# S5 steps and opening of a hybrid decoder re-ordered by engine, one gate DMA each way

## The chip, the cores and the metric

The kernel runs on one core of one Trainium2 chip. Its five engines work in parallel, each through its own queue in program order: TensorE (PE, matmuls), VectorE (DVE), ScalarE (ACT), GpSimd (POOL) and SyncE (SP, which issues DMAs; ACT issues some too). The metric is the device time of one launch in microseconds (us).

## What is computed

One inference step of a two-layer decoder over 592 token columns: 16 meta tokens and 512 prompt tokens, then 8 running sequences of 8 tokens. Layer 0 mixes with an S5 state space model, layer 1 with an RG-LRU; each is followed by a gated causal convolution MLP. The part that matters here is the S5 mixer:

```python
u = x @ w_in                                   # 1024 -> 1024
ug = u.reshape(Bsz, L, 64, 16)                 # 64 groups of 16 channels
bu = einsum('blgh,gph->blgp', ug, bb)          # complex, 64 states a group
s  = associative_scan(s_t = a * s_{t-1} + bu_t)   # complex, a is diagonal
y  = Re(einsum('blgp,ghp->blgh', s, c)) + d_skip * u
gy = gelu(y)
vg = gy @ w_out                                # 1024 -> 2048
out = vg[..., :1024] * sigmoid(vg[..., 1024:])
```

The kernel takes time in chunks of 8: it carries the state over 74 chunk starts (66 of the prompt, one for each sequence), and computes what lies within a chunk with a small Toeplitz matrix per group.

## The kernel before

**Matmuls and weights.** Each f32 product is three matmuls of rounded halves (mm3, lines 150 to 154): high times high, low times high, high times low. Weights come in tiles of 128x1024 by `load` on SP (three buffers); ACT makes the high part (whi, L123), DVE the low part (wlo, L132). `project(m, h)` is half a row of the input projection, 24 matmuls of 296 columns; `projected` copies it out on ACT (L448) and, for the second half, issues its DMA to DRAM from ACT's queue.

**A step.** The S5 mixer runs in eight steps, s = 0 to 7, each over eight groups (128 channels). Its pieces are: `flip_b` (PE, L518) and two copies bt on ACT (L520, L521), which expand B; `spread` (PE, L529) and `operators` (DVE, L537), which make the operator xw; `states` (PE, L593), the input of each chunk; `scans` (DVE, L606 to L614), rotation and scan over the chunks; `turned` (DVE, L622 to L627), rotation back; `ends` (two ACT copies, L631, L632), which saves the end states and puts the running sequences' states in; `carries` (POOL, L545), C times powers of A, tile v with two buffers; `lags` (PE, L554, L557) and `windows` (ACT L564, DVE L565, SP L569), which write the Toeplitz entries to DRAM (td); `fetch_lags` (SP, L573), which reads them back as lagged; `assemble` (ACT, L493 to L496), layouts of B and C; `decays` (ACT L579, then POOL); `outputs` (PE L644 with v and the states, then L648 with lagged and u; ACT gelu L652; one DMA of the gate to DRAM on ACT, L654); `fetch_gy` (L660), which reads the gate back in eight DMAs, four on SP and four on ACT; `split_gy` (ACT L674, DVE L675), its high and low part for the output projection. `phases` (DVE) and `tables` (ACT Sin, L478) make the rotations for two steps at a time, with one buffer between them. `bbar` (DVE, L415 to L417) makes B-bar and `turn_b` (PE, L503) transposes it.

**Order.** From line 697 to line 843 the order is written out by hand (`tc.manual_schedule`): each engine works in the order of the program text. An opening (lines 698 to 766) splits x, computes the parameters (`some(n)` issues n of their small DVE operations) and projects rows 0 to 4. In the loop (767 to 811) step s runs states(s) and scans(s), prepares step s+1, then ends(s-1) and outputs(s-1), fetches gate s-2 and splits gate s-3. Behind the loop (813 to 843) the last outputs run between the first matmuls of the output projection (`glu_part`). PSUM has four tiles, 0 to 3, each of which is free again when its last reader is done; `psum(i)` names one. What follows line 843 (GLU, layer norm, MLP, layer 1) isn't changed.

## Time and profile before

| | us |
|---|---|
| median of 3 runs | 1453.86 (1453.37 to 1454.7) |
| the profiled execution | 1456.19 |
| its span | 1454.1 |
| PE busy in it | 1344.7 (92%) |
| DVE busy | 844.1 (58%) |
| ACT busy | 566.9 (39%) |
| POOL busy | 302.3 (21%) |

The profile is one execution, in us from the start of its span; 2.1 us of the execution lie around the span. A timeline row gives start, duration, engine, line, operation, result and sources, how many were merged (x), and in brackets how long the engine had stood idle and what ended that. Durations in the timeline include the fill of the engine, so the start of the next one says more about the pace. The granted clock is 1.00 at 2.4 GHz and 0.50 at 1.2 GHz.

### The profile page before, as it was taken

How to read it: one execution, taken by the hardware profiler on the slowest of the kernel's cores; microseconds unless marked ns; L12 is line 12 of the kernel's file. 1: busy time of each engine (PE TensorE's matmuls, PEld its weight loads, DVE VectorE, ACT ScalarE, POOL GpSimd, SP SyncE). 2: the span in 40 equal slices, each digit the busy share in tenths (PEclk: the TensorE clock that was granted, in tenths of full speed). 3: DMA queues.
4: the chain of work that ended last, by engine and by line, in shares of the span. 5: the costliest groups of instructions: out<-in, count | busy, mean ns of one | idle time of the engine just before them, and what ended most of it. 6: DMA issues, size and time to landing. Idle time of an engine off the chain costs nothing.

```text
span 1454.1 us, 25622 instructions
## 1 busy us (share of the span) xinstructions
PE 1344.7 (92%) x10680; PEld 1320.4 (91%) x10680; DVE 844.1 (58%) x1421; ACT 566.9 (39%) x934; POOL 302.3 (21%) x368
## 2 busy tenths in 40 slices
PE   6658886999899999999999899999999999999995
PEld 5647876999799999999999799998999999999995
DVE  8355663454865434643554988866856335534546
ACT  4333231333544213431433477844534223323433
POOL 2202221234700000000005823146500000000036
PEclk9869767999999999999999999999999999999998
DMA  6223455531132222222222122321222222222211
GB/s 222 70 73 95 122 113 121 164 102 59 54 105 76 87 73 88 71 77 92 81 79 66 59 88 61 103 99 54 92 88 80 81 87 86 66 96 88 77 52 65
DMA packets 80099, 127.66 MB, mean 88 GB/s; under 512 B 30320, under 2 KB 52976, under 8 KB 79984
## 3 DMA queue, kind: packets, MB, share of 16 engines
q1 hardware_dynamic: 65616, 119.24, 26.5%
q10 hardware_dynamic: 14368, 6.79, 1.9%
q8 instruction: 84, 1.38, 0.4%
q14 instruction: 31, 0.25, 0.1%
HBM read 113.35 MB, written 12.66 MB: 87 GB/s over the span
## 4 chain that ended last, share of the span: by engine, by line
PE 76%; DVE 15%; ACT 5%; issue 2%; ACTq 1%; POOL 1%; DMA 0%; DVEq 0%
PE mm L154 23%; PE mm L152 23%; PE mm L153 23%; PE mm L644 3%; DVE wlo L132 1%; PE mm L648 1%; DVE res L945 1%; DVE lo L951 1%; ACTq L660 1%; DVE res L917 1%; PE mm L593 1%; ACT whi L123 1%; DVE tmp L1311 1%; DVE ini L1308 1%; DVE res L940 1%
## 5 line engine op out<-in xcount | busy, mean ns | idle before, releaser
L152 PE MATMUL mm<-hi,whi 128*128 128x296 f32 (+2 forms) x2816 | 848.1, 301 | 32.0 <-ACT bt L521 10.5
L153 PE MATMUL mm<-lo,whi 128*128 128x296 f32 (+2 forms) x2816 | 847.1, 301 | 16.6 <-DVE lo L951 10.1
L154 PE MATMUL mm<-hi,wlo 128*128 128x296 f32 (+2 forms) x2816 | 845.0, 300 | 2.1 <-DVE wlo L132 2.1
L152 PEld LDWEIGHTS mm<-hi,whi 128*128 128x128 f32 x2816 | 537.5, 191 | 35.5 <-ACT bt L521 11.4
L153 PEld LDWEIGHTS mm<-lo,whi 128*128 128x128 f32 x2816 | 537.3, 191 | 24.7 <-DVE lo L951 14.7
L154 PEld LDWEIGHTS mm<-hi,wlo 128*128 128x128 f32 x2816 | 536.8, 191 | 3.4 <-DVE wlo L132 3.4
L132 DVE TENSOR_TENSOR wlo<-wraw,whi 128x1024 fp32r<-128x1024 f32 (+1 forms) x181 | 226.4, 1255 | 219.4 <-ACT whi L123 218.8
L123 ACT ACTIVATE whi<-wraw 128x1024 fp32r<-128x1024 f32 (+1 forms) x188 | 194.6, 1039 | 301.5 <-PE mm L153 293.7
L1133 POOL TENSOR_TENSOR tmp<-tmp,hist 128x16 f32<-128x16 f32 x88 | 20.5, 235 | 697.4 <-DVE tmp L1130 697.4
L1128 DVE SCALAR_TENSOR_TENSOR tmp<-mm,sm,tmp 128x512 f32<-128x512 f32 (+2 forms) x176 | 132.0, 750 | 0.0
L1132 ACT ACTIVATE stg<-mm 128x18 f32<-128x18 f32 x88 | 16.4, 186 | 185.5 <-DVE tmp L1130 185.5
L1180 DVE TENSOR_TENSOR res<-mm,res 128x296 f32<-128x296 f32 (+3 forms) x48 | 26.0, 558 | 80.4 <-PE mm L154 80.4
L1123 ACT ACTIVATE tmp<-mm,sm 128x592 f32<-128x592 f32 (+1 forms) x88 | 72.2, 823 | 0.0
L545 POOL TENSOR_TENSOR v<-cq,ap 128x512 f32<-128x512 f32 x32 | 40.5, 1295 | 79.9 <-PE mm L644 35.8
L1139 DVE TENSOR_TENSOR tmp<-tmp 128x592 f32<-128x592 f32 (+1 forms) x44 | 33.7, 767 | 38.7 <-ACT tmp L1138 38.7
L169 DVE TENSOR_TENSOR lo<-tmp,hi 128x592 fp32r<-128x592 f32 (+2 forms) x48 | 36.6, 763 | 29.6 <-ACT hi L168 29.6
L878 POOL TENSOR_TENSOR s<-s,res 128x296 f32<-128x296 f32 (+2 forms) x45 | 41.8, 931 | 57.3 <-DVE res L1086 27.9
L974 POOL TENSOR_SCALAR res<-res,sm 128x592 f32<-128x592 f32 (+1 forms) x24 | 49.1, 2065 | 7.0 <-DVE lo L951 7.0
L879 POOL TENSOR_TENSOR s<-s,tmp 128x296 f32<-128x296 f32 (+2 forms) x53 | 50.4, 955 | 0.2 <-ACT tmp L874 0.2
L168 ACT ACTIVATE hi<-tmp 128x592 fp32r<-128x592 f32 (+2 forms) x48 | 33.1, 690 | 43.9 <-DVE tmp L1139 30.0
L644 PE MATMUL mm<-sx,v 64*128 64x74 f32 x512 | 40.1, 327 | 10.5 <-ACT sx L632 10.5
L644 PEld LDWEIGHTS mm<-sx,v 64*128 64x128 f32 x512 | 38.7, 239 | 11.9 <-ACT sx L632 11.4
(276 smaller groups left out, 1197.4 us busy)
## 6 DMA issues: line engine op xcount, KB each, us to landing
wraw<-in_wup SPq DMA_DIRECT2D x88, 512.0 KB, 3.4
wraw<-in_wdn SPq DMA_DIRECT2D x32, 448.0 KB, 3.3
wraw<-in_w5o SPq DMA_DIRECT2D x16, 512.0 KB, 4.4
wraw<-in_wdn SPq DMA_DIRECT2D x16, 512.0 KB, 3.6
wraw<-in_wri SPq DMA_DIRECT2D x16, 512.0 KB, 3.5
wraw<-in_w5i SPq DMA_DIRECT2D x8, 512.0 KB, 5.4
td<-lagsb SPq DMA_DIRECT2D x8, 512.0 KB, 3.4
lagged<-td SPq DMA_DIRECT2D x8, 512.0 KB, 4.2
```

Of the source, the lines that this page charges most:

```text
L123: A.activation(hi[:, 0:kk, :], t[:, 0:kk, :], AF.Copy)
L132: eng.tensor_tensor(lo[:, 0:kk, :], t[:, 0:kk, :], hi[:, 0:kk, :].bitcast(F32), op=ALU.subtract)
L152: T.matmul(out, hi[:, k, :], xh, start=start, stop=False)
L153: T.matmul(out, hi[:, k, :], xl, start=False, stop=False)
L154: T.matmul(out, lo[:, k, :], xh, start=False, stop=stop)
L545: G.tensor_tensor(v[:, m], c[:, a, :, None, :].to_broadcast(sh), b[:, NQ * q:NQ * q + NQ, 1:CH + 1, None].to_broadcast(sh), op=ALU.mult)
L644: T.matmul(at_(g, i), v[rows, m, i].rearrange("p d h -> p (d h)"), sx[rows, m // 2, i, 0:NK], start=i + m == 0, stop=False, skip_group_che ...
L878: G.tensor_tensor(self.s1[:, cs_], RES[0][:, cs_] if m == 1 else self.s1[:, cs_], z, op=ALU.add)
L879: G.tensor_tensor(self.s2[:, cs_], self.s2[:, cs_], sq[:, cs_], op=ALU.add)
L974: G.tensor_scalar(z, z, bm, None, op0=ALU.add)
L1123: A.activation(acc[:, d0:NT], X(d0, NT), AF.Identity, scale=w[2], bias=fcb[:, l, m:m + 1])
L1128: V.scalar_tensor_tensor(acc[:, a:TP], X(a - sh, TP - sh), w[k], acc[:, a:TP], op0=ALU.mult, op1=ALU.add)
```

## The change

It re-orders the S5 mixer's opening, loop and end, and alters five things in it:

- flip_b is parted into its matmuls and its two ACT copies (`flipped`), which move to the start of the next step; split_gy is parted into `gy_hi` and `gy_lo`.
- ends(s-1) becomes the first work of step s on ACT; whi, windows, assemble, gate conversions and decays follow it; lags and windows move ahead of outputs.
- v gets the layout (h, d) instead of (d, h), so lags reads it with a step, and the rows of outputs come out as (channel, time in chunk). The matrix read back is put in the same order by a new ACT instruction a step, `toeplitz`; lagged has one buffer instead of two, toe has one.
- The gate is then read back by one DMA on SP instead of eight on SP and ACT.
- PSUM tiles are dealt out anew: projections alternate between 0 and 3, lags moves from 2 to 0, flip_b to 1 for the first three.

In the opening, bbar(2,5) and the weight splits come before other work of their engines, and the projections are placed anew: (5,0) to (6,1) in step 0, row 7 in step 1. At the end, glu_part(0,1) comes after the last outputs.

```diff
-                ps = psum(3 if m < PJ0 and h else 0)[:, 0:HALF]
+                ps = psum((0, 3)[(len(PD) + (m > 4)) % 2])[:, 0:HALF]
+                PD.append(m)
...
                 BT[q] = s5.tile([P, 3, NQ * P], F32, tag="bt", name="bt")
-                pt = psum(0).rearrange("p (r c) -> p r c", r=2)
+                pt = psum(0 if q > 2 else 1).rearrange("p (r c) -> p r c", r=2)
...
+                FL[q] = pt
+
+            def flipped(q):
+                pt = FL.pop(q)
                 A.activation(BT[q][:, 0:2], pt, AF.Copy)
                 A.activation(BT[q][:, 2], pt[:, 1], AF.Copy, scale=-1.0)
...
-                VV[q] = v = s5.tile([P, 4, NQ, CH, 16], F32, tag="v", name="v", bufs=2)
-                sh = [P, NQ, CH, 16]
+                VV[q] = v = s5.tile([P, 4, NQ, 16, CH], F32, tag="v", name="v", bufs=2)
+                sh = [P, NQ, 16, CH]
                 for m, (a, b) in enumerate(((0, apr), (1, api), (0, nai), (1, apr))):
-                    G.tensor_tensor(v[:, m], c[:, a, :, None, :].to_broadcast(sh),
-                                    b[:, NQ * q:NQ * q + NQ, 1:CH + 1, None].to_broadcast(sh), op=ALU.mult)
+                    G.tensor_tensor(v[:, m], c[:, a, :, :, None].to_broadcast(sh),
+                                    b[:, NQ * q:NQ * q + NQ, None, 1:CH + 1].to_broadcast(sh), op=ALU.mult)
...
-                pl = psum(2)
+                pl = psum(0 if q < DM - 1 else 2)
...
-                                 v[:, n, i, 0:CH - 1, :].rearrange("p d h -> p (d h)"), start=n == 0, stop=n == 3)
+                                 v[:, n, i, :, 0:CH - 1].rearrange("p h d -> p d h"), start=n == 0, stop=n == 3)
...
-                lagged = s5.tile([P, NG, P], F32, tag="lagged", name="lagged", bufs=2)
+                lagged = s5.tile([P, NG, P], F32, tag="lagged", name="lagged")
                 nc.sync.dma_start(lagged, TOE[q].rearrange("g p c -> p g c"))
                 TOE[q] = lagged
+
+            def toeplitz(q):
+
+                toe = s5.tile([P, NG, P], F32, tag="toe", name="toe")
+                A.activation(toe.rearrange("p g (h d) -> p g h d", h=16),
+                             TOE[q].rearrange("p g (d h) -> p g h d", d=CH), AF.Copy)
+                TOE[q] = toe
...
-                            T.matmul(at_(g, i), v[rows, m, i].rearrange("p d h -> p (d h)"), sx[rows, m // 2, i, 0:NK],
+                            T.matmul(at_(g, i), v[rows, m, i].rearrange("p h d -> p (h d)"), sx[rows, m // 2, i, 0:NK],
...
             def fetch_gy(q):
-
-                gd = by_group(GD.pop(q)).rearrange("(j h) g k -> g h j k", j=CH)
-                for g in range(NG):
-                    (nc.sync, nc.scalar)[g % 2].dma_start(RES[q][16 * g:16 * g + 16, :].rearrange("p (j k) -> p j k", j=CH), gd[g])
+                nc.sync.dma_start(RES[q], GD.pop(q))
...
-            def split_gy(q, eng=V):
+            def gy_views(q):
+                return RES[q].rearrange("p (j k) -> p k j", j=CH), [t.rearrange("p (k j) -> p k j", j=CH) for t in GY[q]]
+
+            def gy_hi(q):
                 GY[q] = hlpair()
-                gy = RES[q].rearrange("p (j k) -> p k j", j=CH)
-                hi, lo = (t.rearrange("p (k j) -> p k j", j=CH) for t in GY[q])
+                gy, (hi, lo) = gy_views(q)
                 A.activation(hi, gy, AF.Copy)
-                eng.tensor_tensor(lo, gy, hi.bitcast(F32), op=ALU.subtract)
+
+            def gy_lo(q):
+                gy, (hi, lo) = gy_views(q)
+                V.tensor_tensor(lo, gy, hi.bitcast(F32), op=ALU.subtract)
+
+            def split_gy(q):
+                gy_hi(q)
+                gy_lo(q)
...
+            def projection(m, h):
+                project(m, h)
+                projected(m, h)
...
             with tc.manual_schedule():
                 some(24)
@@ -701,133 +713,149 @@
                     if k == 0:
                         load(1)
                         convert_next()
-                    some(2)
+                    some(1)
                     if k == 3:
                         load(2)
                 project(0, 0)
                 convert_next()
+                project(1, 0)
                 for k in range(DM):
                     split_x(k, 1)
-                    some(3)
+                    some(2)
+                load(3)
                 nc.sync.dma_start(bB, s5bc[:, :, 0:128].rearrange("q p (a c) -> p q a c", a=2))
+                projected(0, 0)
+                project(0, 1)
+                projected(1, 0)
+                some(20)
+                convert_next()
+                load(4)
                 nc.sync.dma_start(sp1, s5p[:, S5_COLS["sre"][0]:S5_COLS["sim"][1]].rearrange(
                     "p (r n s) -> p r n s", r=2, s=8))
-                load(3)
+                load(5)
                 fetch_c(0)
                 fetch_c(1)
-                load(4)
-                projected(0, 0)
-                project(0, 1)
+                project(1, 1)
+                projected(0, 1)
+                some(20)
                 convert_next()
-                projected(0, 1)
-                load(5)
-                project(1, 0)
-                projected(1, 0)
-                some(40)
-                project(1, 1)
-                convert_next()
+                some(200)
                 projected(1, 1)
-                some(200)
+                projection(2, 0)
                 bbar(0, 2)
-                project(2, 0)
+                projection(2, 1)
+                load(6)
                 turn(aT, [apw[:, 2 * n:2 * n + 2].rearrange("p q r i j -> p (q r i j)") for n in range(DM // 2)])
-                projected(2, 0)
                 turn_b(0, 2)
                 convert_next()
-                load(6)
-                project(2, 1)
-                projected(2, 1)
+                project(3, 0)
+                flip_b(0)
+                projected(3, 0)
+                flipped(0)
+                spread(0)
                 phases(0)
-                flip_b(0)
-                spread(0)
                 operators(0)
-                project(3, 0)
-                projected(3, 0)
+                convert_next()
+                load(8)
+                project(3, 1)
                 fetch_u(0)
-                fetch_u(1)
                 tables(0)
                 assemble(0)
+                carries(0)
+                decays(0)
+                projected(3, 1)
                 G.tensor_tensor(sm8[:, 0], sp1[:, 0], m8b, op=ALU.mult)
                 G.tensor_tensor(sm8[:, 1], sp1[:, 1], m8b, op=ALU.mult)
-                carries(0)
-                decays(0)
-                project(3, 1)
-                projected(3, 1)
+                bbar(2, 5)
+                assemble(1)
+                flip_b(1)
+                flipped(1)
+                convert_next()
+                fetch_c(2)
                 nc.sync.dma_start(sm, smp)
-                fetch_c(2)
-                convert_next()
-                bbar(2, 5)
-                flip_b(1)
-                assemble(1)
+                projection(4, 0)
                 turn_b(2, 5)
-                project(4, 0)
-                projected(4, 0)
-                project(4, 1)
-                projected(4, 1)
+                projection(4, 1)
                 for s in range(DM):
                     last = s == DM - 1
-                    if s:
-                        run(fetch_u, s + 1)
-                        run(fetch_c, s + 2)
+                    run(ends, s - 1)
+                    run(fetch_u, s + 1)
+                    run(fetch_c, s + 3)
                     load(min(at["conv"] + 3, 12))
-                    states(s)
-                    scans(s)
+                    if 1 < s < DM - 1:
+                        flipped(s + 1)
+                    if at["conv"] < 12:
+                        convert_hi(at["conv"] + 1)
                     if last:
                         lags(s)
                         windows(s)
-                    else:
-                        project_next()
+                    states(s)
+                    if not last:
+                        lags(s)
+                    scans(s)
+                    if not last:
+                        windows(s)
+                    run(assemble, s + 2)
+                    run(toeplitz, s - 1)
+                    run(gy_hi, s - 3)
+                    run(decays, s + 1)
+                    if not last:
                         spread(s + 1)
                         operators(s + 1)
-                        projected_next()
-                    run(ends, s - 1)
+                    fetch_lags(s)
+                    if s == 0:
+                        projection(5, 0)
+                        convert_next()
+                        projection(5, 1)
+                    if s == 1:
+                        projection(7, 0)
                     run(outputs, s - 1)
                     run(fetch_gy, s - 2)
                     turned(s)
-                    if not last:
-                        run(carries, s + 1)
-                        lags(s)
-                        windows(s)
-                    fetch_lags(s)
+                    run(carries, s + 1)
+                    if s == 1:
+                        projection(7, 1)
+                    run(flip_b, s + 2)
                     if at["conv"] < 12:
-                        convert_next()
+                        convert_lo(at["hi"])
                     if s == 0:
+                        flipped(2)
                         phases(1)
                         tables(1)
+                        convert_next()
+                        projection(6, 0)
+                        bbar(5, 8)
                         phases(2)
                         tables(2)
-                        bbar(5, 8)
+                        projection(6, 1)
+                        turn_b(5, 8)
                         phases(3)
                         tables(3)
-                        turn_b(5, 8)
-                    run(flip_b, s + 2)
-                    run(assemble, s + 2)
-                    run(decays, s + 1)
-                    project_next()
-                    projected_next()
-                    run(split_gy, s - 3)
+                    run(gy_lo, s - 3)
                     if s == 6:
                         GL[0, 0] = psum(0), 0
                         glu_part(0, 0, 4, False)
 
                 a, b = DM - 2, DM - 1
-                if at["conv"] < 12:
+                while at["conv"] < 12:
                     convert_next()
+                ends(b)
                 glu_part(0, 0, 5, False)
-                GL[0, 1] = psum(1), 0
-                glu_part(0, 1, 5, False)
-                ends(b)
-                split_gy(a - 1)
+                gy_hi(a - 1)
                 fetch_gy(a)
                 residual(0, 4)
+                toeplitz(b)
                 outputs(b)
+                gy_lo(a - 1)
                 load(15)
+                GL[0, 1] = psum(1), 0
+                glu_part(0, 1, 6, False)
                 GL[1, 0] = psum(2), 0
                 glu_part(1, 0, 6, False)
                 glu_part(0, 0, 6, False)
-                glu_part(0, 1, 6, False)
+                gy_hi(a)
                 fetch_gy(b)
-                split_gy(a)
+                gy_lo(a)
                 GL[1, 1] = psum(3), 0
                 glu_part(1, 1, 6, False)
                 for m in range(2):
```

## Rows read from the trace of the kernel before

**Rows 1.** Windows: stretch, its length, each engine's busy us (instructions), granted clock, DMA share, GB/s.

```profile
133.30:235.30 102.00, 84.05 (x1186) 78.72 (x1184) 60.91 (x74) 28.75 (x80) 27.15 (x30) 0.77 0.45 106
235.30:262.90 27.60, 19.48 (x197) 18.68 (x198) 6.89 (x12) 3.61 (x6) 0.00 (x0) 0.81 0.64 173
262.90:349.70 86.80, 86.80 (x638) 86.56 (x637) 40.82 (x89) 32.41 (x52) 26.09 (x29) 1.00 0.32 102
```

**Rows 2.** Chain of waits, 200 to 212 us: start, us, what.

```profile
201.95 0.38 ACTq L654
...
205.86 0.92 ACT bt L520
...
208.99 1.10 ACT hi L674
...
210.28 0.27 ACT sx L632
```

**Rows 3.** Timeline of PE, then of DVE and ACT, in the opening and step 0.

```profile
64.07 0.87 PE L503 MATMUL mm<-ident,bb 128*128 128x128 f32 x3 [11.38 <-DVE bb L417]
...
95.24 0.88 PE L503 MATMUL mm<-ident,bb 128*128 128x128 f32 x3 [11.26 <-DVE ph L461]
...
86.56 0.16 DVE L461 COPY ph<-pv 128x8 int32<-128x8 int32 x1
...
98.47 1.33 ACT L478 ACTIVATE res<-pc 128x296 f32<-128x296 int32 x2
```

**Rows 4.** Timeline of PE, step 1 (full clock), then step 6.

```profile
113.37 3.80 PE L644 MATMUL mm<-sx,v 64*128 64x74 f32 x64
117.10 2.01 PE L648 MATMUL mm<-u,lagged 128*128 128x74 f32 x16
...
119.18 0.95 PE L557 MATMUL mm<-v,bst 128*32 128x112 f32 x32
120.06 1.16 PE L518 MATMUL mm<-bB,sel 64*128 64x128 f32 x16
...
204.57 2.27 PE L593 MATMUL mm<-u,xw 128*64 128x74 f32 x64
...
210.60 6.85 PE L644 MATMUL mm<-sx,v 64*128 64x74 f32 x64 [2.66 <-ACT sx L632]
217.38 3.69 PE L648 MATMUL mm<-u,lagged 128*128 128x74 f32 x16
```

**Rows 5.** Timeline of DVE in step 0 (one row) and step 5, then of POOL.

```profile
83.69 0.46 DVE L627 TENSOR_TENSOR sx<-t 128x296 f32<-128x296 f32 x1
...
189.95 1.19 DVE L675 TENSOR_TENSOR lo<-res,hi 128x592 fp32r<-128x592 f32 x1 [3.01 <-ACT hi L674]
...
197.34 0.77 DVE L622 TENSOR_TENSOR t<-t,res 128x592 f32<-128x592 f32 x1
198.03 1.63 DVE L623 TENSOR_TENSOR t<-t,res 128x592 f32<-128x592 f32 x1
...
200.82 1.31 DVE L627 TENSOR_TENSOR sx<-t 128x296 f32<-128x296 f32 x1
...
197.63 5.42 POOL L545 TENSOR_TENSOR v<-cq,ap 128x512 f32<-128x512 f32 x4 [8.59 <-PE mm L644]
```

**Rows 6.** The page's groups: busy us, mean ns of one, idle before.

```profile
L132 DVE TENSOR_TENSOR wlo<-wraw,whi 128x1024 fp32r<-128x1024 f32 (+1 forms) x181 | 226.4, 1255 | 219.4 <-ACT whi L123 218.8
...
L168 ACT ACTIVATE hi<-tmp 128x592 fp32r<-128x592 f32 (+2 forms) x48 | 33.1, 690 | 43.9 <-DVE tmp L1139 30.0
```

**Rows 7.** Windows of 2 us, columns as in rows 1.

```profile
122.00:124.00 2.00, 0.96 (x7) 0.96 (x8) 0.98 (x1) 1.99 (x9) 0.00 (x0) 1.00 1.11 268
...
206.00:208.00 2.00, 1.94 (x44) 1.66 (x38) 1.12 (x1) 1.99 (x8) 0.00 (x0) 1.00 0.99 266
```

**Rows 8.** The page's DMA issues: count, KB of one, us to landing.

```profile
td<-lagsb SPq DMA_DIRECT2D x8, 512.0 KB, 3.4
lagged<-td SPq DMA_DIRECT2D x8, 512.0 KB, 4.2
```

More of the change, by code (lines that the diff above doesn't have):

```diff
@@ L34 @@
 CENTER = 4
-PJ0 = 5
 S5_COLS = dict(lre=(0, 32), lim=(32, 64), ls=(64, 96), dsk=(96, 104), sre=(104, 360), sim=(360, 616),
@@ L426, in trunk @@
                 G.memset(t[:, :, :, 0:1], 0.0)
+            PD = []
             U, XW, CC, BST, VV, BT, TOE = {}, {}, {}, {}, {}, {}, {}
-            UT, UD, GD, PJ, PH, D0, ST = {}, {}, {}, {}, {}, {}, {}
+            UT, UD, GD, PJ, PH, D0, ST, FL = {}, {}, {}, {}, {}, {}, {}, {}
             def by_group(dram):
@@ L685, in convert_next @@
                 convert_lo(at["conv"] + 1)
-            proj = [(m, h) for m in range(PJ0, DM) for h in (0, 1)]
-            def project_next():
-                if proj:
-                    project(*proj[0])
-            def projected_next():
-                if proj:
-                    projected(*proj.pop(0))
+            def projection(m, h):
+                project(m, h)
+                projected(m, h)
             with tc.manual_schedule():
```

## The prediction

> **What bounds the kernel now.** I first cut the span into stretches. From 262.9 us on TensorE (PE) is full: 638 matmuls in 86.8 us, so 0.136 us for one of 296 columns and 3.3 us for the 24 of half a projection [rows 1]. The diff touches nothing there, so whatever is won must be won before 262.9. In the recurrence, 133.3 to 235.3, PE is busy for 84 of 102 us, but at a mean granted clock of 0.77, so much of that busy time is itself stretched [rows 1]. I mark the steps by the first matmul of outputs (L644), which belongs to the step before: from 133.3 to 235.3 five steps took 102.0 us, 20.4 each [rows 1].
>
> The chain of waits says what a step is made of. After the gate's gelu, ScalarE (ACT) issues the gate DMA at 201.95 and four fetches behind it, then works through the next steps' conversions: bt at 205.86, assemble, decays, hi of split_gy at 208.99. Only then come the two copies of ends, at 210.28 [rows 2], and only they let PE go on. So the step is ACT's 9 us and PE's 10.5 us in series: outputs waits for ends, ends stands at the tail of ACT's queue, and that queue was blocked until outputs' gelu. Before the steps PE stands still twice for transposes of bbar, for 11.38 and 11.26 us [rows 3].
>
> **The opening.** The first stop is bbar(2,5), which on VectorE (DVE) is queued behind a weight split, whose whi stands behind tables(0) on ACT; it also runs beside carries on GpSimd (POOL). The change puts that split before tables(0), and bbar(2,5) behind it on a DVE that is then free: I take back 11.4 us. Project (2,1) moves into PE's 2.3 us wait before the first turn_b, and the projections after the first stop no longer run at half clock for their first 3 us (1.6 us). Sum: 15 us, states(0) at about 57. The parameter arithmetic that keeps DVE busy until 33 us has the same instructions, so splitting x with one parameter step between instead of two wins nothing here. The sm8 products move behind carries(0) on POOL; they then end near 57, when scans(0) is ready: nothing, or 2 us.
>
> In step 0 the phases on DVE and the Sin tables on ACT still take turns, since they share one buffer: 86.56 to 99.80 in the trace, 13.2 us [rows 3]. Interleaved with two weight splits and four projections, I count 19 us from turned(0) at 68.5, so 87.4. Behind it ACT does ends(0), whi, windows, assemble, toeplitz, decays and the copy of project(7,0), 6 us: outputs(0) may start at 93, not 113.4 [rows 4]. **Gain to here 20 us.** Until outputs(1), PE has L644 3.7, L648 1.95, project(7,1) 3.3, flip 1.1, then bt(3) on ACT 1.5, lags 1.2 and spread 1.1, like flip's 1.1 [rows 2, 4], plus about 1 for semaphores: 15 us against 19.9, 5 us. PE has however just idled before outputs(0); at half clock L644 and L648 take 6.85 and 3.65 [rows 4]. I keep half of it: 1.5 us. **Gain 21.5 us.**
>
> **A steady step.** Let T be the end of turned(s-1). ACT does ends first (T+0.5), then bt(s+1) (T+2.0). PE has done states(s); lags(s) needs the PSUM tile that bt frees, so it runs T+2.0 to 3.3, spread to 4.4, L644 to 8.1, L648 to 10.1, flip to 11.2, states(s+1) to 13.4 [rows 4]. DVE does the two low parts, scans, the windows' small operation, operators, turned. Of these, scans to turned took 191.1 to 202.1 in the trace, 11.1 us; low part of the gate 1.2 [rows 5], the small one 0.2, and while weights are still being split 1.2 more [rows 6]: starts overlap by a tenth, so 13.6 us in two steps, 12.4 in three. So DVE becomes the bound, with PE idle for 2.3 us or less in one piece: five steps are 2 x 13.6 + 3 x 12.4 = 64.4 us instead of 102.0, **37.6 us**.
>
> Costs inside. toeplitz adds one ACT instruction of 128x1024 with 64-byte steps: hi of the gate, also strided, takes 1.10 for 592 elements [rows 2], the packed hi 0.69 [rows 6], so 1.2 to 1.9 for 1024. I take 1.9, since it is strided too; ACT then ends it at about T+6.6, under L644, which ends at 8.1: nothing. Its cover gone, it costs up to 1.9 a step. The moving operand of lags now has 32-byte steps; no row prices PE for that. By the same two rows it is 1 to 1.6 times 0.95 [rows 4], or 0 to 0.6 us more, within PE's idle time: nothing. The one gate fetch takes four issues off ACT, some 2.2 us a step, and is on SP behind fetch_lags, which waits for td; gy_hi comes a step later, so nothing waits. carries still begins when L644 frees v [rows 5], and lags(s+1) needs it at L644's end + 5.5; flip and states cover that. Its four products have other broadcast axes but the same 512 elements, and fetch_c and load are as many issues on SP as before, ahead of td: nothing each.
>
> carries meets turned as it does now: L623 took 1.63 us beside POOL and its twin L622, begun before POOL, 0.77; L627 1.31 against 0.46 in step 0. With L626 like L627 that is 2.5 of turned's 4.8 us [rows 5]. The 4.8 stands in the sum; if carries drifts off, it is 2.5 less a step, 12 in all. The Trainium skill (SBUF — State Buffer, Who interferes with whom) states that one of a VectorE operation with two SBUF inputs and a GpSimd one that reads SBUF blocks fully until the other has finished. Four operations each waiting for a whole carries instruction of 1.3 us would make turned 7.1 us and five steps 11 us longer; the row, with 4.8, shows less. As a rival it gives 1409.
>
> **The clock** is the largest unknown. PE kept 1.00 through an idle 1.8 us, from flip's end at 121.2 to 123.0 [rows 4, 7], but 2.66 us before 210.60 sufficed for a cold L644 [rows 4]. A step's gap of 2.3 us lies between. A drop costs 3.1 on L644, 1.7 on L648 and, until states, some 1.3 more: 6 us. For five steps I allow 1.5 drops, 9 us, which leaves 28.5.
>
> **The end.** outputs(6) to the end of outputs(7) is 27.6 us now [rows 1]. After: 5.7 for outputs(6), 2 until gate 4's low part, 0.8 for glu, 5.7 for outputs(7), 1.9 waiting for toeplitz(7): 16.1. glu_part(0,1) with its 30 matmuls moves behind it, 4.1 us. 27.6 - 16.1 - 4.1 = 7.4, of which I keep 6. The fetches of gates 6 and 7 are hidden: 18.8 us of other glu matmuls follow. The four-tile output tail named in the change's words has no line in the diff: nothing.
>
> **Sum:** 21.5 + 28.5 + 6 = 56 us. The profiled execution took 1456.2 (span 1454.1 and 2.1 around it), 2.3 over the median of 1453.9. 1456.2 - 56 - 2.3 gives **1398 us**. With no drop it is 70 us (1384), with turned uncontended 80 (1374).
>
> **Rivals.**
> (1) The clock falls in every step. PE is then the bound: 6.85 + 3.65 for outputs, 4.6 for lags and spread at twice their rows, then warm 1.1 for flip and 2.2 for states, 18.4 a step [rows 4], so 92 instead of 102; with 21.5 before and 3 after, a gain of 34.5, 1419 us. For it: a gap near the critical length in every step; against: the clock was up again by 206, after flip and states [rows 7], and they now run straight on into lags and spread. The Trainium skill (TensorE: Matmul & The Clock Gate, HAM oscillation) describes a kernel whose bursts between waits each start throttled.
> (2) The round trip td to lagged to toeplitz bounds the step: lagged now has one buffer, and on ACT gelu and the next ends stand behind toeplitz. 3.4 and 4.2 us to landing [rows 8] and 1 for the two issues, from T+6.6: T+15.2, while toeplitz is reached at T+13.6+4.7. Slack 3 us; if both landings double, 4.5 us are lost in each of five steps: 1420.
> (3) The other side: PE stays at half clock from the opening to outputs(7). Each step is then 21.6 us of PE work (10.5, twice 1.2, 1.1, 1.1 and 2.2), over the present 20.4, and half a projection 6.6. From 47 us on, where project(3,1) ends, that is 8 halves, 53 us, 8 steps, 173, and 10 for glu and transposes: outputs(7) ends at 283, with the moved 4.1 us 24 later than now: 1478. It decides only if the projections stay cold too; against it speaks that they ran at 1.00 just before 124 [rows 7].
>
> **How the numbers follow.** Forecast 0.67, drops in every step 0.16, the port 0.06, the round trip 0.05, slower 0.04, nothing moved 0.02. Range 1374 to 1428: the bound of the forecast below; above, rivals 1 and 2 and 8 us more, should my count of step 0 be short by two in five. A measurement tells about 0.2% (3 us): faster 0.94, same 0.02, slower 0.04.
>
> **What would show it.** Right: ends just behind turned on ACT, L644 spaced 12 to 14 us, DVE busy over 80% there, no four ACT fetches, PE's wait before L644 gone. Wrong: L644 of 6.9 us in most steps (1), L648 waiting for toeplitz over 3 us (2), states(0) after 65 us (opening).

## The result, and the profile after

The changed kernel takes 1402.9 us (median of four runs, 1398.4 to 1412.4), the kernel before in the same rounds 1454.3 us: a ratio of 0.966, with a 95% interval of 0.961 to 0.971. A second set of five runs gave 1410.7 us against 1456.6, 0.968 (0.965 to 0.971). The forecast was 1398 us, within 1374 to 1428. The profiled execution of the changed kernel took 1403.1 us, its span 1401.3; that of before 1456.2 and 1454.1, so 53.1 us went. The nine runs of the changed kernel lie in two groups, at 1398 to 1403 and at 1411 to 1412 us; where a difference below is taken from 1402.9, it is some 8 us smaller against the second set.

The line numbers have moved: outputs is L656 and L660 now, states L605, lags L559 and L562, spread L534, flip L519, ends L643 and L644, bt L525 and L526, hi and lo of the gate L685 and L689, the weights' whi and wlo L122 and L131, toeplitz L584, the four products of turned L634 to L639, carries L550.

The windows of the trace, with the columns of [rows 1], cut where the prediction cut them: states(0) to outputs(0), to outputs(1), to outputs(6), to the end of outputs(7).

```profile
54.14:91.82 37.68, 30.59 (x397) 27.69 (x396) 31.59 (x65) 22.33 (x51) 6.57 (x9) 0.95 0.43 139
91.82:114.01 22.19, 21.68 (x249) 20.28 (x249) 4.93 (x10) 6.32 (x15) 4.26 (x4) 0.69 0.27 72
114.01:185.52 71.51, 62.86 (x1114) 56.60 (x1112) 60.64 (x72) 36.42 (x78) 28.87 (x30) 0.98 0.54 140
185.52:203.90 18.38, 16.67 (x171) 16.07 (x167) 8.47 (x13) 5.51 (x8) 0.00 (x0) 0.75 0.66 210
```

The third row answers the first of [rows 1]: the same five steps take 71.5 us instead of 102.0, VectorE (DVE) works for 60.6 us of it as against 60.9, now 85% of the stretch, and TensorE's (PE's) granted clock is 0.98 instead of 0.77. The second row is the one that got worse: PE is busy for all but 0.5 us, at a mean clock of 0.69.

ScalarE (ACT) in a steady step, as a timeline; it answers [rows 2]:

```profile
140.61 1.99 ACT L584 ACTIVATE toe<-lagged 128x1024 f32<-128x1024 f32 x1
142.51 1.24 ACT L685 ACTIVATE hi<-res 128x592 fp32r<-128x592 f32 x1
...
145.79 0.73 ACT L664 ACTIVATE gu<-mm 128x296 f32<-128x296 f32 x2 [1.70 <-PE mm L660]
146.55 0.43 ACTq L666 DMA_DIRECT2D gd<-gu  x1
150.37 0.27 ACT L643 ACTIVATE hold<-sx 128x72 f32<-128x72 f32 x1 [3.85 <-DVE sx L639]
150.66 0.26 ACT L644 ACTIVATE sx<-sp 128x64 f32<-128x64 f32 x1
150.83 1.01 ACT L525 ACTIVATE bt<-mm 128x1024 f32<-128x1024 f32 x1
151.73 0.59 ACT L526 ACTIVATE bt<-mm 128x512 f32<-128x512 f32 x1
```

ends (L643) here waits for turned's last product on DVE, and for nothing on its own queue: ACT has 3.85 us to spare in front of it. In step 5 it stands behind gelu and the gate DMA and starts at 162.30, 2.2 us after turned's end at 160.13. What trailed at the end of ACT's queue leads it, with bt behind.

DVE and GpSimd (POOL) at the same place, and the two low parts of the step before, against [rows 5] and [rows 6]:

```profile
134.91 2.13 DVE L131 TENSOR_TENSOR wlo<-wraw,whi 128x1024 fp32r<-128x1024 f32 x1
136.96 2.07 DVE L689 TENSOR_TENSOR lo<-res,hi 128x592 fp32r<-128x592 f32 x1
...
145.41 0.77 DVE L634 TENSOR_TENSOR t<-t,res 128x592 f32<-128x592 f32 x1
146.09 1.67 DVE L635 TENSOR_TENSOR t<-t,res 128x592 f32<-128x592 f32 x1
147.79 1.25 DVE L638 TENSOR_TENSOR sx<-t 128x296 f32<-128x296 f32 x1
148.97 1.36 DVE L639 TENSOR_TENSOR sx<-t 128x296 f32<-128x296 f32 x1
150.25 1.18 DVE L689 TENSOR_TENSOR lo<-res,hi 128x592 fp32r<-128x592 f32 x1
...
158.49 0.77 DVE L635 TENSOR_TENSOR t<-t,res 128x592 f32<-128x592 f32 x1
...
144.32 5.69 POOL L550 TENSOR_TENSOR v<-cq,ap 128x512 f32<-128x512 f32 x4
...
159.69 5.45 POOL L550 TENSOR_TENSOR v<-cq,ap 128x512 f32<-128x512 f32 x4
```

Three of turned's four products are stretched beside carries, to 1.67, 1.25 and 1.36 us, as in [rows 5]; the first, L634, is not, though by the profile carries has begun. The low parts now run beside carries too in some steps, 2.13 and 2.07 us where 1.2 was in the sum. In step 5 turned is all but done when carries begins at 159.69; L635 then takes 0.77 us and turned 2.3 in all.

PE from outputs(3) to outputs(4), against [rows 4], and the transposes of the opening, against [rows 3]. Here and in the expectations a step is named by the outputs at its end, so this is step 4:

```profile
50.44 0.49 PE L504 MATMUL mm<-ident,bb 128*128 128x128 f32 x3
...
77.93 0.52 PE L504 MATMUL mm<-ident,bb 128*128 128x128 f32 x3 [4.01 <-DVE ph L462]
...
140.02 3.80 PE L656 MATMUL mm<-sx,v 64*128 64x74 f32 x64
143.74 2.01 PE L660 MATMUL mm<-u,toe 128*128 128x74 f32 x16
145.68 1.16 PE L519 MATMUL mm<-bB,sel 64*128 64x128 f32 x16
146.77 2.27 PE L605 MATMUL mm<-u,xw 128*64 128x74 f32 x64
152.37 0.32 PE L559 MATMUL mm<-cq,bst 128*32 128x16 f32 x16 [3.33 <-ACT bt L526]
152.52 1.82 PE L562 MATMUL mm<-v,bst 128*32 128x112 f32 x32
154.27 1.16 PE L534 MATMUL mm<-aT,sel 32*128 32x128 f32 x16
155.36 3.80 PE L656 MATMUL mm<-sx,v 64*128 64x74 f32 x64
```

The first transposes wait for nothing (11.38 us before), the second for 4.01 (11.26). In the step, outputs no longer waits; the wait stands before lags, which needs the PSUM tile that bt frees. It is 3.33 us here, the longest such wait, and the next outputs still takes 3.80 us, that is, at full clock. The windows say the same, against [rows 7]; the third is the whole of step 5:

```profile
148.00:150.00 2.00, 1.05 (x34) 0.89 (x28) 2.00 (x2) 0.00 (x0) 2.00 (x2) 1.00 1.14 233
150.00:152.00 2.00, 0.00 (x0) 0.00 (x0) 2.00 (x3) 1.60 (x4) 0.01 (x1) 1.00 1.26 214
...
155.36:167.30 11.94, 11.94 (x226) 10.76 (x225) 9.36 (x15) 7.68 (x15) 5.57 (x6) 1.00 0.61 166
```

In step 5, with turned undisturbed, PE is busy for all 11.94 us at full clock and DVE for 9.36: that step is PE's. The three before it are DVE's, which is busy for 13.3 of 13.6, 12.4 of 12.5 and 14.9 of 15.3 us.

The page's DMA issues give td 3.4 and lagged 4.2 us to landing, as in [rows 8].

**Where the 53 us are.** Up to outputs(0) 113.37 - 91.82 = 21.6; to outputs(1) 19.9 before and 22.2 now, so 2.3 back; five steps 102.0 - 71.5 = 30.5; outputs(6) to the end of outputs(7) 27.6 - 18.4 = 9.2, of which 4.1 are matmuls that moved behind it, so 5.1. That is 55; 2 us are lost again later, which I have not followed.

### The profile page after: what moved, and what is told of

Same layout as the page of the kernel before. It is cut to its first block, busy times and chain, and to the rows that moved or that the text cites. A ratio compares the mean times of both kernels' runs of the same rounds, so it can differ in the third digit from the quotient of the medians.

```text
span 1401.3 us, 25545 instructions
## 1 busy us (share of the span) xinstructions
PE 1333.1 (95%) x10680; PEld 1308.4 (93%) x10680; DVE 840.2 (60%) x1421; ACT 582.7 (42%) x942; POOL 301.1 (21%) x368
## 4 chain that ended last, share of the span: by engine, by line
PE 76%; DVE 17%; ACT 4%; issue 2%; POOL 1%; DMA 0%; SPq 0%; DVEq 0%; ACTq 0%
PE mm L152 24%; PE mm L153 24%; PE mm L151 24%; DVE wlo L131 2%; DVE res L973 1%; DVE lo L979 1%; PE mm L656 1%; DVE xw L542 1%; DVE res L945 1%; PE mm L660 1%; PE mm L605 1%; DVE t L635 1%; ACT res L479 1%; DVE res L968 1%; ACT whi L122 1%
## 5 line engine op out<-in xcount | busy, mean ns | idle before, releaser
L131 DVE TENSOR_TENSOR wlo<-wraw,whi 128x1024 fp32r<-128x1024 f32 (+1 forms) x181 | 228.2, 1265 | 220.0 <-ACT whi L122 219.3
L122 ACT ACTIVATE whi<-wraw 128x1024 fp32r<-128x1024 f32 (+1 forms) x188 | 194.5, 1039 | 302.5 <-PE mm L152 297.5
L906 POOL TENSOR_TENSOR s<-s,res 128x296 f32<-128x296 f32 (+2 forms) x45 | 41.8, 930 | 60.9 <-DVE res L1114 31.2
L550 POOL TENSOR_TENSOR v<-cq,ap 128x512 f32<-128x512 f32 x32 | 42.5, 1359 | 49.8 <-ACT cq L494 41.1
L902 ACT ACTIVATE tmp<-res 128x296 f32<-128x296 f32 (+2 forms) x56 | 24.0, 445 | 58.0 <-DVE res L1208 24.7
L1206 DVE SCALAR_TENSOR_TENSOR res<-res,mm 128x592 f32<-128x592 f32 (+1 forms) x16 | 12.2, 762 | 59.2 <-PE mm L153 59.2
```

Source lines behind the costliest of these rows:

```text
L122: A.activation(hi[:, 0:kk, :], t[:, 0:kk, :], AF.Copy)
L131: eng.tensor_tensor(lo[:, 0:kk, :], t[:, 0:kk, :], hi[:, 0:kk, :].bitcast(F32), op=ALU.subtract)
L550: G.tensor_tensor(v[:, m], c[:, a, :, :, None].to_broadcast(sh), b[:, NQ * q:NQ * q + NQ, None, 1:CH + 1].to_broadcast(sh), op=ALU.mult)
L906: G.tensor_tensor(self.s1[:, cs_], RES[0][:, cs_] if m == 1 else self.s1[:, cs_], z, op=ALU.add)
```

## The experiments

**Is the lead of ends enough, and is it needed?** The prediction's main step was that outputs waits for ends and ends stands at the tail of ACT's queue. First only that was moved, in the kernel before (step 7 has a call of its own behind the loop):

```diff
-                    run(ends, s - 1)
                     run(outputs, s - 1)
                     run(fetch_gy, s - 2)
                     turned(s)
+                    if not last:
+                        ends(s)
```

> The kernel before with one edit: ends(s) is issued right behind turned(s), so on ScalarE it stands ahead of that step's weight, bt, assemble, decays and gate copies instead of behind them. Theory A (the step was ScalarE's 9 us and PE's 10.5 us in series because ends stood at the queue's tail): a step becomes VectorE's sum of some 13.6 us instead of 20.4; over six steps about 40 us less, 1414 us, with PE's wait before the outputs gone. Rival (the position of ends matters only together with the other moves, since bt, the eight fetches or the cold clock set the step just as well): steps stay near 18 us or more and the time above 1438 us.

Measured: 1451.1 us, 0.997 of before (0.996 to 0.998). The rival holds; 5 us of 53 come. The trace (line numbers of before) shows the wait before outputs gone and the ring closed elsewhere. ACT, DVE and PE in step 5, in order of time:

```profile
188.87 1.23 ACT L674 ACTIVATE hi<-res 128x592 fp32r<-128x592 f32 x1
...
190.13 1.20 DVE L675 TENSOR_TENSOR lo<-res,hi 128x592 fp32r<-128x592 f32 x1 [3.33 <-ACT hi L674]
...
200.85 0.42 PE L554 MATMUL mm<-cq,bst 128*32 128x16 f32 x16 [6.23 <-DVE xw L537]
...
202.98 0.27 ACT L631 ACTIVATE hold<-sx 128x72 f32<-128x72 f32 x1 [7.61 <-DVE sx L627]
```

ACT's tail still holds hi of the gate; DVE has the gate's low part ahead of scans and waits 3.33 us for hi; so scans, operators and turned are late, lags waits 6.23 us for operators, since lags and spread share a PSUM tile, and ends itself waits 7.61 us for turned. Moving one instruction out of a serial ring shows the next one in it.

Then the reverse, in the changed kernel: ends behind toeplitz, hi and decays on ACT, everything else new.

```diff
                 for s in range(DM):
                     last = s == DM - 1
-                    run(ends, s - 1)
...
                     run(gy_hi, s - 3)
                     run(decays, s + 1)
+                    run(ends, s - 1)
```

> The changed kernel with ends(s-1) moved behind bt, whi, windows, assemble, toeplitz, the gate's high part and decays on ScalarE, everything else as it is. Theory A: the outputs' first matmul begins some 4.5 us later in each step, steps go from about 13.5 to 17 or 18 us, 1428 to 1435 us. Rival (the gain is the other re-ordering): within 5 us of the changed kernel, 1400 to 1408 us.

Measured: 1451.0 us, 0.997 (0.996 to 0.999). All of the gain but 5 us is gone, and more than theory A allowed: the lead of ends is necessary. The copies it was put behind are some 5 us of ACT, but the steps are 21 to 24 us, for PE now waits 1.7 to 4.5 us in front of outputs and, but for the last of them, comes back at half clock:

```profile
140.12 7.11 PE L656 MATMUL mm<-sx,v 64*128 64x74 f32 x64 [4.46 <-ACT sx L644]
...
150.78 2.08 PE L519 MATMUL mm<-bB,sel 64*128 64x128 f32 x16
152.80 3.88 PE L605 MATMUL mm<-u,xw 128*64 128x74 f32 x64
```

From outputs to flip every matmul is at half speed, and most of states (7.11 against 3.80, 2.08 against 1.16, 3.88 against 2.27). This is what rival (1) described. The Trainium skill (TensorE: Matmul & The Clock Gate, HAM oscillation) tells of bursts that each start throttled; these rows agree.

**What the gate's new way is worth.** The new order with the old v layout, no toeplitz, two lagged buffers, and eight gate fetches, alternately from SyncE (SP) and ACT:

```diff
-                nc.sync.dma_start(RES[q], GD.pop(q))
+                gd = by_group(GD.pop(q)).rearrange("(j h) g k -> g h j k", j=CH)
+                for g in range(NG):
+                    (nc.sync, nc.scalar)[g % 2].dma_start(RES[q][16 * g:16 * g + 16, :].rearrange("p (j k) -> p j k", j=CH), gd[g])
```

> The changed kernel with the old layout of v, two buffers for lagged, no toeplitz, and the gate fetched in eight DMAs again; the new order stays. Theory A (VectorE bounds the step, so none of this lies on its path): steps within 0.5 us of the changed kernel, a few us lost at the end where the last two gates are fetched: 1400 to 1408 us. Rival (four fetch issues on ScalarE, 2.2 us a step, still hold up the next ends): 1415 us or more. The other way: lags with a packed operand takes 0.95 us instead of 1.82 and toeplitz's 1.95 us is gone; if these were on the path it would be 1390 us.

Measured: 1426.0 us, 0.980 (0.978 to 0.983), 23 us above the changed kernel's 1402.9 and 15 above its second set: the rival. ACT's timeline shows why:

```profile
142.03 0.38 ACTq L666 DMA_DIRECT2D gd<-gu  x1
142.45 6.10 ACTq L671 DMA_DIRECT2D res<-gd  x4
148.60 0.27 ACT L643 ACTIVATE hold<-sx 128x72 f32<-128x72 f32 x1 [6.60 <-DMA res<-gd]
```

The four issues hold ACT's queue for 6.10 us here and for 2.2 to 6.6 us in the other steps, and ends is what stands behind them. Three of the five outputs that follow run at half clock. To tell the issues from the transfers and from the layouts, one word was changed in that kernel, all eight issues to SP:

```diff
-                    (nc.sync, nc.scalar)[g % 2].dma_start(
+                    nc.sync.dma_start(
```

> As e3_old_gate (the layouts, buffers and eight gate fetches of before inside the new order), but all eight fetches are issued by SyncE, none by ScalarE. Theory A (in e3 the four issues on ScalarE stood between gelu and ends for 6.1 us, and with ends leading, all of it fell on the path that sets the end: that is what e3 lost): 1398 to 1410, ends within 1.5 us of gelu. Rival (it is the eight transfers themselves, or the eight issues wherever they stand, since SyncE now holds td and lagged behind them): 1418 or more.

Measured: 1405.8 us, 0.967 (0.965 to 0.969), between the changed kernel's two sets. ends follows the gate DMA at once:

```profile
137.12 0.38 ACTq L666 DMA_DIRECT2D gd<-gu  x1
137.82 0.27 ACT L643 ACTIVATE hold<-sx 128x72 f32<-128x72 f32 x1 [0.73 <-ACT gu L664]
...
130.82 11.91 SPq L671 DMA_DIRECT2D res<-gd  x8
```

On SP the eight issues may take 11.91 us and cost nothing that the runs can tell. So 20 us were four DMA issues on the wrong queue, half clock that followed from them included. The one large gate DMA, the transposed v and toeplitz together are worth no more than that one word, as far as the runs can tell; one by one they weren't tried, and since this kernel's lags is packed too, gains and losses among them could cancel. The Trainium skill (DMA: Bandwidth & Descriptors, Rules for kernel authors) says that spreading DMAs over several engines saves only the issuing time; here the issuing time decided.

**The strided operand of lags, and the clock.** In the changed kernel lags reads v with 32-byte steps and takes 1.82 us, not 0.95 [rows 4]. Packed again:

```diff
-                                 v[:, n, i, :, 0:CH - 1].rearrange("p h d -> p d h"), start=n == 0, stop=n == 3)
+                                 v[:, n, i].rearrange("p h d -> p (h d)")[:, 0:P - 16], start=n == 0, stop=n == 3)
```

> The changed kernel, but lags reads the first 112 elements of v packed instead of with a step of 32 bytes (so the entries within a chunk are in the wrong order; the amount of work is the same). Expected: the 32 matmuls of lags take 0.95 us instead of 1.82. Theory A (hidden in PE's idle time, VectorE bounds the step): 0 to 3 us less, 1400 to 1403 us. Rival (they lie on the path of every step): 7 us less, 1396 us.

Measured: 1415.6 us (1408.8 to 1416.0), 0.971 (0.968 to 0.974). Both theories missed: with less work, the kernel is some 13 us slower than the first set of the changed kernel and 5 slower than the second; one of its four runs (1408.8) lies within the range of those nine. lags does take 0.95 us, but:

```profile
124.68 0.32 PE L559 MATMUL mm<-cq,bst 128*32 128x16 f32 x16 [2.80 <-ACT bt L526]
...
128.26 7.11 PE L656 MATMUL mm<-sx,v 64*128 64x74 f32 x64
...
143.85 0.95 PE L562 MATMUL mm<-v,bst 128*32 128x112 f32 x32
```

bt comes from DVE and ACT and is ready when it was; PE just arrives earlier, idles for 2.80 us instead of 1.54, and the next outputs runs at half clock. Two of the five steps are cold so. My new theory: the step is DVE's, PE's spare time is paid for in clock. Two runs test it, the changed kernel once more and the packed lags issued twice:

> The changed kernel as it is, on the same chip and in the same rounds as the three edits beside it, so that a few microseconds between them can be read. Theory A (its time moves with the number of stretches at half clock): 1398 to 1412 over its runs, and those with a lower mean granted clock are the longer ones. Rival (the spread has another source, for example transfers): the mean clock of the runs doesn't order their times.

> As e4_lags_packed (the lags' moving operand packed, so its entries within a chunk are in the wrong order), but the 32 packed matmuls are issued twice, first into columns of the same PSUM tile that nobody reads. TensorE's time for lags is then 2 x 0.95 = 1.9 us a step, as the strided ones took (1.82), and nothing else differs from e4. Theory A (e4 was slower only because TensorE, with 0.9 us less to do in a step that VectorE sets, idled longer and came back at half clock): 1398 to 1407, at least 8 us under e4's 1415.6, TensorE's clock at 1.00 between outputs(1) and outputs(6). Rival (something else in the packed reading costs e4 its 12 us, and work that nobody needs only adds time): 1415 or more.

```diff
+                for to in (pl[:, 512 + 16:512 + P], pl[:, 16:P]):
                     for n in range(4):
                         for i in range(NQ):
-                            T.matmul(pl[32 * i:32 * i + 32, 16:P], bst[:, n // 2, i, :],
+                            T.matmul(to[32 * i:32 * i + 32], bst[:, n // 2, i, :],
```

Measured: packed lags twice, 1404.1 us (1402.4 to 1405.7), 0.965 (0.963 to 0.966). Useless work on PE took 11 us off. One expectation was too neat: the clock did fall once after a wait for bt, of 3.21 us, but was up again before outputs. The changed kernel's second set gave 1410.7 us. Its nine runs form two groups: four of 1398.4 to 1403.1 us with a mean clock of 0.980 to 0.984, five of 1410.7 to 1412.4 with 0.973 to 0.976. The profiled execution of the second set belongs to the longer group, and its step 4 has the very wait of the first:

```profile
153.87 0.32 PE L559 MATMUL mm<-cq,bst 128*32 128x16 f32 x16 [3.33 <-ACT bt L526]
154.02 1.82 PE L562 MATMUL mm<-v,bst 128*32 128x112 f32 x32
155.77 2.08 PE L534 MATMUL mm<-aT,sel 32*128 32x128 f32 x16
157.78 7.11 PE L656 MATMUL mm<-sx,v 64*128 64x74 f32 x64
```

The steps before it agree with the first trace to 0.1 us, and the wait is 3.33 us in both. Once the clock stayed, once it fell, and then outputs(3) to outputs(5) took 16.3 and 18.6 us instead of 15.3 and 11.9. So the same wait cost 8 us or nothing, by something that neither trace shows. The run with eight issues on SP has both cases in one execution, two steps apart:

```profile
122.71 0.32 PE L559 MATMUL mm<-cq,bst 128*32 128x16 f32 x16 [2.62 <-ACT bt L526]
...
155.54 0.32 PE L559 MATMUL mm<-cq,bst 128*32 128x16 f32 x16 [2.63 <-ACT bt L526]
```

After the first, outputs took 7.11 us, after the second 3.80. A gap of that length can't be priced as hit or miss from one profile. That this wait makes the whole second group was seen in one profile of it only; the runs below, with a shorter wait, bear it out.

**The opening.** One part of it undone, the weight split after operators(0) put behind tables(0) again:

```diff
                 operators(0)
-                convert_next()
...
                 projected(3, 1)
+                convert_next()
```

> Undo of one part of the opening: the weight split that follows operators(0) stands behind tables(0) and the copy of projection (3,1) again, ahead of bbar(2,5), as it did before the change. Theory A (this order is what took TensorE's 11.4 us wait for bbar(2,5) away): states(0) 8 to 12 us later than 54.1, total 1410 to 1415. Rival (the wait went because bbar(2,5) now precedes the split of the next weights and GpSimd's carries, so that the split's place matters little): states(0) within 4 us of 54.1, total 1400 to 1407.

Measured: 1416.4 us, 0.971 (0.968 to 0.973), against 1410.7 and 0.968 (0.965 to 0.971) for the changed kernel in the same rounds. The intervals overlap, but both kernels have two groups of runs, and each of this one lies some 6 us above that of the other: 1407.6 against 1401.2, 1416.6 against 1410.7; a fifth run, 1410.9, lies between them. PE's transposes and states(0):

```profile
56.14 0.88 PE L504 MATMUL mm<-ident,bb 128*128 128x128 f32 x3 [5.53 <-DVE bb L416]
```

A wait of 5.53 us is back, and states(0) begins at 62.1, 6.4 later than at 55.6 in the changed kernel beside it. It lies between the two theories: the place of the split explains about half of the 11.4 us that I gave to it.

**A version that beats both.** Two stretches of the changed kernel still idle: the transposes of bbar(5,8) in step 0 (4.01 us, above), and step 6, where glu_part(0,0) waits for the low part of gate 3, 3.35 us, and step 6 takes 18.2 us.

```diff
                         projection(6, 1)
+                        projection(7, 0)
                         turn_b(5, 8)
...
-                    if s == 1:
-                        projection(7, 0)
...
-                        glu_part(0, 0, 4, False)
+                        glu_part(0, 0, 3, False)
```

> Two edits for the two stretches in which the changed kernel still falls to half clock or idles. First: project(7,0) stands ahead of the transposes of bbar(5,8) in step 0 instead of ahead of outputs(0) in step 1. Second: in step 6 glu_part(0,0) takes three gates instead of four, so that it doesn't wait for the low part of gate 3. Theory A: outputs(0) begins at 86 to 88 instead of 91.8, with less of it at half clock, and step 6 is 4 us shorter: 1388 to 1395. Rival (project(7,0) only moves from one place that TensorE must fill to another, VectorE's scans and turned set the time of outputs(1), and glu's matmuls come back behind outputs(7)): 1400 to 1406.

Measured: 1399.8 us (1392.9 to 1401.3), 0.960 (0.958 to 0.963), 10.8 below the changed kernel in the same rounds, a little less good than expected and again in two groups. To fill the wait for bt with work that is needed, spread was put ahead of lags:

```diff
                     states(s)
                     if not last:
+                        spread(s + 1)
                         lags(s)
...
                     if not last:
-                        spread(s + 1)
                         operators(s + 1)
```

> One move in the changed kernel: spread(s+1), which TensorE issues behind lags(s), stands ahead of it, so that its 1.16 us fall into TensorE's wait for bt (1.52 us in step 2, 3.33 us in step 4) and no longer behind it. Theory A (the 8 us between the changed kernel's runs are one fall to half clock after the 3.33 us wait of step 4; a shorter wait is not followed by one): all runs 1396 to 1405, no cluster at 1410. Rival (the clock falls by some other cause, or spread now holds back lags, windows and the round trip behind them): runs at 1410 still, or all above 1405.

> The same move on top of e7_both (project(7,0) earlier, three gates in step 6), whose runs lay at 1393 to 1394 and at 1400 to 1401. Theory A: all runs 1387 to 1395. Rival as for e10_spread_first: runs at 1400 still.

> e11_both_spread with the second half of project (7,1) in step 2 instead of step 1. In e7_both outputs(0) to outputs(1) took 22.2 us, with VectorE idle for 12.3 of them, since TensorE had outputs(0) and this half at half clock ahead of states(2). Theory A (the step that follows outputs(0) is TensorE's, the ones behind it are VectorE's, so 3.3 to 6.6 us of TensorE's work move from the one to the other's slack): 4 to 6 us under e11_both_spread. Rival (TensorE has no 3.3 us to spare in step 2, or its wait for the copy of the projection costs as much): within 2 us of e11_both_spread or above.

Measured, with before at 1455.9: spread alone 1395.8 us (1394.6 to 1398.1), 0.959 (0.958 to 0.960); on top of the two edits 1387.6 (1386.8 to 1388.4), 0.953 (0.952 to 0.955); with project(7,1) in step 2 besides 1385.5 (1383.5 to 1387.5), 0.952 (0.951 to 0.953). The second group is gone in all three, in four or five runs each. The same wait in step 4 of the first of them, and the five steps of the last:

```profile
146.16 0.32 PE L559 MATMUL mm<-cq,bst 128*32 128x16 f32 x16 [1.73 <-ACT bt L526]
```

```profile
101.72:166.93 65.21, 63.79 (x1134) 57.10 (x1130) 59.77 (x72) 36.00 (x82) 30.41 (x30) 1.00 0.58 157
```

3.33 us became 1.73, and the five steps take 65.2 us at a clock of 1.00, with project(7,1) in them. Part of the gain of spread lies in the opening: outputs(0) takes 3.80 us there instead of 6.56. The last move gave 2.1 us where 4 to 6 were expected; its interval overlaps that of the run it builds on, so it isn't shown to be faster than it.

## Why the prediction was right, point by point

- **Outputs waits for ends, ends at the tail of ACT's queue.** Right, but as half of the cause. With the other changes ends' lead is worth 48 us (1451.0 against 1402.9; 40 against the second set), alone it is worth 5. The prediction's own ring for the new step had the other conditions in it (low part behind scans, lags in another PSUM tile, ACT without the four issues), and it took them as given. Of these only ACT's issues were tried by themselves.
- **The gate fetches, "some 2.2 us a step off ACT ... nothing waits".** This step was wrong in kind. The four issues took 2.2 to 6.6 us a step in the new order, and once ends leads they stand right before it: 20 us. The sum came out because the new step was built without them; the part's own worth was put at nothing.
- **Opening, 20 us to outputs(0).** 21.6 measured; states(0) at 54.1, not 57, outputs(0) at 91.8, not 93. Of the 11.4 us for the split's place 6.4 were shown. As to the rest, bbar(2,5) itself took 6.1 us on DVE before, beside carries, 3.7 with the split late and 2.1 in the changed kernel; this wasn't tried apart.
- **outputs(0) to outputs(1), 1.5 us kept.** Wrong in sign, -2.3. outputs(0) took 6.56 us and project(7,1) ran cold behind it; the drop that I halved came in full in both profiled executions of the changed kernel. (Half of the 5 us would also have been 2.5, not 1.5.)
- **Five steps, 64.4 us of DVE and 9 for the clock.** 71.5 measured, 73.4 forecast, by other parts: the near hit is partly luck. DVE is the bound, as said, in steps 2 to 4; scans to turned took 11.3 us in steps 2 and 4, against 11.1. Step 5 is PE's, 11.9 us. The steps were 13.6, 12.5, 15.3, 11.9 and 18.2 us, not all 12 to 14. The clock fell in the profiled execution only in step 6; in the profile of the longer group it cost 8 us more, so the 9 us stand as an upper end. Instead two steps grew, step 4 to 15.3 us, since low parts beside carries took 2.1 us for 1.2, and step 6 to 18.2, since glu waited for gate 3's low part.
- **turned beside POOL.** 5.05 us against 4.8 in the sum where it met carries, and not the 7.1 of that rival: 1.67 us for L635 beside carries, 0.77 before it. carries is stretched too: its four products take 4.26 us at 98.46, where DVE is idle, and 5.69 here, so 1.3 us for one wait was too much. In step 3 it took 4.0 us, in step 5 2.3, so carries did drift off in part, as the prediction allowed for; but there the low part met carries instead (2.03 us), and PE set the step. (By the prediction's own terms the undisturbed case is 70 + 12 = 82 us, not 80, and with 2.3 us alone and four waits of 1.3 the rival's 7.1 is 7.5.)
- **toeplitz, 1.2 to 1.9.** 1.99 in the step shown, under outputs, and never waited for in these five steps, as said. A kernel without it took 1405.8, but that one has packed lags and eight fetches besides, so its worth alone isn't shown. **lags, 0 to 0.6 more.** 0.87 more, out of the bound: ACT's rows were no guide to PE's. It was hidden as said, and more than that: with it taken away the runs were longer.
- **The end, 6 us.** 5.1. The four-tile tail, for which the diff has no line, was nothing.
- **Rivals.** (1), the clock falling in every step, is what happens when ends is late, and in one step of five in the slower group. (2): outputs' second part never waited for toeplitz. (3) did not come near.

## What to carry to other kernels

In a serial ring over several engines, the place of one instruction is worth little alone and much together with the others: list what stands ahead of it on its queue, DMA issues too, and give issues to the engine that has time. Once another engine sets the step, a shorter operation on TensorE can lose time, because its longer idle time is followed by half clock; fill the wait with work that is needed, by changing the order, before making the work smaller. A wait at the edge of a clock fall makes two groups of run times, so run such a kernel often enough to see both.

## What the runs showed of the hardware

- A matmul of 112 columns whose moving operand has 32-byte steps: 1.82 us for 32 of them, against 0.95 packed, at the same clock.
- TensorE's clock after an idle 3.33 us in the same place of the same kernel: 1.00 in one execution, half in another. Within one execution of another kernel it fell after 2.62 us and not after 2.63. After 2.40 us it fell in outputs(0) of the changed kernel.
- The same four DMA issues held ScalarE's queue for 2.17 to 4.89 us a step in the kernel before and for 2.22 to 6.56 us in the new order; eight held SyncE's for up to 11.91 us.
- A VectorE product of 592 elements a partition took 1.67 us while carries ran on GpSimd and 0.77 us before carries began, in the same kernel.
